# Attention slots: other places for splits, fillers and copies; last norm: gain and 1/rms in one operation

## The chip, the cores and the metric

The kernel runs on one core of one Trainium2 chip. The metric is the device time in microseconds (us), as the median of several runs. TensorE (PE) multiplies matrices into banks of PSUM. VectorE (DVE) and ScalarE (ACT) do the work by element, GpSimd (POOL) the reduction over partitions and some transfers, and SyncE (SP) starts most transfers. Each engine works through its own queue in order, and an instruction that waits holds up those behind it.

## The reference

A decoder trunk of two layers on 1024 tokens of width 1024, in f32. Layer 0 mixes by a short gated convolution, layer 1 by dilated attention with 16 heads of 64 and three branches. Each is followed by a SwiGLU, and a last RMSNorm ends it.

```python
def rms_norm(x, g):
    xf = x.astype(jnp.float32)
    y = xf * lax.rsqrt(jnp.mean(xf * xf, axis=-1, keepdims=True) + EPS)
    return (y * g.astype(jnp.float32)).astype(x.dtype)
...
    for i in range(DEPTH):
        h = rms_norm(x, mix_norm[i])
        j = i // N_MIXERS
        if i % N_MIXERS == 0:
            x = x + short_conv_mixer(h, conv_w_in[j], conv_kernel[j], conv_w_out[j])
        else:
            x = x + dilated_attention_mixer(h, attn_w_qkv[j], attn_w_out[j], rel_bias)
        h = rms_norm(x, ffn_norm[i])
        x = x + swiglu(h, ffn_w_gate[i], ffn_w_up[i], ffn_w_down[i])
    return rms_norm(x, final_norm)
```

In the attention, each branch (windows 128, 512 and 2048 at strides 1, 4 and 16) has scores q k / 8 plus a bias by distance, a softmax, and values. The branches are joined with weights by their sums of exponentials, which is the same as one softmax over the keys of all three.

## The kernel before, in words

Every f32 factor is split into two parts, hi and lo, and a product is three matmuls: hi hi, hi lo, lo hi (L372 to L374 in `product`). `split` makes the parts: ACT copies hi (L144), DVE subtracts for lo (L145).

The attention is a loop over 17 slots, n = 0 to 16. Slot n issues the scores of head n, the softmax of head n, the values of head n - 1, and 15 steps of a list of fillers, other matmuls that keep PE supplied. What is issued first stands first in each engine's queue: the order of the calls is the order of the work.

- `scores`: PE multiplies into seven banks (L1573, L1574). DVE adds the bias and writes the scores to four tiles, `lf`, `lh`, `ld` and `lp` (L1584, L1593, L1610, L1615), takes maxima into `m` (L1598 to L1624), and POOL reduces them over the partitions to `mb` (L1627).
- `softmax` has five steps, for lf, lh, ld and lp twice: DVE subtracts the maximum (L1635), ACT takes the exponential (L1636).
- `values` multiplies the exponentials by the values into two banks (L1646). The rows of one half hold the sums of exponentials: ACT takes their logarithm into `z` (L1669), and copies the rows of the other half into `o` (L1670).
- `finish` (for a pair of heads, two slots later) takes exp(-z) (L1677). `attended` multiplies o by it (L1710) and stores the page.
- The fillers stand in `FILL`: ("v", g) is a group of value tiles (L1516 to L1518, ACT copies with L1521), ("qk", g) is a pair of heads' projections. A result of a projection is emitted in four parts: DVE scales it into `kq` (L1139 or L1141), ACT copies `kq_hi` (L1144), DVE subtracts `kq_lo` (L1147). Behind the list stands the output product of the attended pages 0 to 3 (L372 to L374), which DVE adds to x (L491).
- In slot 12 (LAG - 1) these attended pages, loaded back as `oin`, are split by the generator `halves`, which the slot steps as `hook`.

PSUM has eight banks that are given out in turn, so the product that takes a bank waits until DVE or ACT has read what was put into it eight turns earlier.

The last norm runs in the kernel's last stage, on pieces of 512, 256 and 256 columns. `each` squares a tile on ACT and multiplies it by its gain on ACT (L1935). DVE adds the squares (L1940). When the sum of a piece is known, `scaled` multiplies each of the eight tiles by 1/rms on DVE (L1944) and stores it. For the last piece PE sums the squares (L1958), and spreads 1/rms over the partitions by a product with a diagonal (L1965, L1973): the last eight products read it from PSUM.

Of the kernel before, what the change touches and what calls it, by code (L numbers as in the profile page):

```python
# [12 lines left out]
AF = mybir.ActivationFunctionType  # L13
ALU = mybir.AluOpType
# [6 lines left out]
H = 16  # L21
KT = D // 128
FT = DF // 128
HALF = 512
# [22 lines left out]
SOFT = 4  # L47
# [1 line left out]
AO_WIDE = 5  # L49
AO = 4  # L50
LAG = 13
FILL = (("v", 0), ("v", 1), ("v", 2), ("qk", 6), ("qk", 7), ("v", 3))
DEEP_ORDER = (1, 2, 5, 6, 7, 3, 4)


# [39 lines left out]
def view(t, off, dims):  # L95
    return bass.AP(tensor=t.tensor, offset=t.offset + off, ap=[t.ap[0]] + [list(d) for d in dims])
# [3 lines left out]
def trunk(ctx: ExitStack, tc: tile.TileContext, x, gains_in, cwi, ck, cwo, wqkv, wo, relb,  # L100
          wg, wu, wd, oneh, ident, out):
    nc = tc.nc
# [6 lines left out]
    def page(name, dt=F32):  # L109
        return pages.tile([128, 1024], dt, name=name, tag="page", bufs=PAGES)  # L110
# [6 lines left out]
    def bank():  # L117
        return psum.tile([128, 512], F32, name="bank", tag="bank")

    def half(h):  # L120
        return slice(h * HALF, (h + 1) * HALF)
# [225 lines left out]
    add_units(QK, QK_PAIRS, lambda u, n: wqkv[(KT, 0)[n] + u])  # L347
    for kind, g in FILL:
        if kind == "v":
# [27 lines left out]
    def run(*gens):  # L377
        for _ in zip(*gens):
            pass
        for g in gens:  # L380
            for _ in g:
                pass
# [12 lines left out]
    X = [None] * KT  # L395
# [1068 lines left out]
    def load_bias(h):  # L1464
        t = scope["pool"].tile([128, L1 + L2], F32, name="bias", tag="bias", bufs=2)
        base = tables.offset + h * G3
        nc.sync.dma_start(t[:, 0:L1], bass.AP(tensor=tables.tensor, offset=base, ap=[[1, 8], [A1, 16], [1, L1]]))
        nc.sync.dma_start(t[:, L1:L1 + L2], bass.AP(tensor=tables.tensor, offset=base + G0,
                                                    ap=[[1, 32], [A2, 4], [1, L2]]))
        return t  # L1470
# [5 lines left out]
    def blk(j):  # L1476
        return (j // 4) * HALF + (j % 4) * 8

    def attention(norm, qk):
# [150 lines left out]
        def softmax(st):  # L1630
            lf, lh, ld, lp, mb = (st[n] for n in ("lf", "lh", "ld", "lp", "mb"))
            for dst, m in ((lf, mb), (lh, mb[:, HALF:]), (ld, mb),
                           (view(lp, 8, [[32, 16], [1, 24]]), view(mb, 8, [[32, 16], [1, 24]])),
                           (lp[:, HALF:], mb[:, HALF:])):
                nc.vector.tensor_tensor(out=dst, in0=dst, in1=m, op=ALU.subtract)  # L1635
                nc.scalar.activation(dst, dst, AF.Exp)  # L1636
                yield

        def values(p, a, st):
            lf, lh, ld, lp = (st[n] for n in ("lf", "lh", "ld", "lp"))  # L1640
            acc = [bank(), bank()]
            kd = [[128, 4], [1, 32]]
            b1 = [[32, 16], [1, 8]]

            def mm(ih, off, dims, u, rhs, first=False, last=False):
                nc.tensor.matmul(view(acc[ih], off, dims), vx[:, u, 64 * a:64 * a + 128], rhs,  # L1646
                                 start=first, stop=last)

            for ih in range(2):
                for r4 in range(4):  # L1650
                    mm(ih, r4 * 32, kd, 8 + r4, view(lf, ih * HALF + r4 * 32, kd), first=r4 == 0)
                    if r4 % 2:
                        yield
            for r4 in range(4):
                mm(1, r4 * 32, kd, 12 + r4, view(lh, r4 * 32, kd))
                if r4 % 2:
                    yield
            for j in range(8):
                off = (j % 4) * 8
                mm(j // 4, off, b1, j, view(ld, blk(j), b1), last=False)  # L1660
                if j:
                    mm(j // 4, off, b1, j - 1, view(lp, blk(j), b1), last=j % 4 == 3)
                yield
            o, z = st["o"], st["z"]
            n0 = slice(64 * a, 64 * a + 64)
            z0 = slice(64 - 64 * a, 128 - 64 * a)
            for ih in range(2):
                s = slice(ih * HALF, (ih + 1) * HALF)
                nc.scalar.activation(z[n0, s], acc[ih][z0], AF.Ln)  # L1669
                nc.scalar.activation(o[n0, s], acc[ih][n0], AF.Copy)  # L1670
            yield

        def finish(p):
# [42 lines left out]
        def slot(n, dense, ndense, late=0, hook=iter(())):  # L1716

            def other(k):
                for _ in range(k):
                    next(dense, None)  # L1720

            p, a = divmod(n, 2)
            if n < H:
                new = dict(bias=bias.pop(n))
                sc = scores(p, a, new)
            else:
                sc = iter(())
            if n + 1 < H:
                load_kq(n + 1)
                bias[n + 1] = load_bias(n + 1)  # L1730
            if n:
                q, b = divmod(n - 1, 2)
                if b == 0:
                    OZ[q] = page("o"), page("z")
                old = live.pop(n - 1)
                old.update(o=OZ[q][0], z=OZ[q][1])
                pv = values(q, b, old)
            else:
                pv = iter(())
            extra = later = iter(())  # L1740
            lagged = n <= LAG
            if n + 1 < H:
                later = classes(n + 1)
            if lagged and a and p:
                ending.append(finish(p - 1))
            used = 0
            if lagged:
                for i in range(8):
                    next(sc, None)
                    if n or i % 2:  # L1750
                        other(1)
                        used += 1
                    if a and ending and i == 0:
                        run(ending.pop())
                run(sc)
            else:
                if a == 0 and not late:
                    other(1)
                    used += 1
                for i in range(8):  # L1760
                    next(sc, None)
                    next(pv, None)
                    next(pv, None)
                    if i >= late and i % 2 == 0:
                        other(1)
                        used += 1
                run(sc)
                run(pv)
                if a == 0:
                    extra = finish(p - 1)  # L1770
                if a == 0 and n < H:
                    load_values(p)
            left = max(ndense - used, 0)
            for i in range(8):
                next(pv, None)
                next(pv, None)
                if i == (2 if n > LAG + 1 else 5):
                    attended()
                if not lagged and (i < FIN0 or i > SOFT):
                    next(extra, None)  # L1780
                if i in (1, 2):
                    next(later, None)
                if i == (3 if lagged else SOFT):
                    if n < H:
                        live[n] = new
                        run(softmax(new))
                if i >= SOFT:
                    next(hook, None)
                other(left * (i + 1) // 8 - left * i // 8)
            run(pv)  # L1790
            run(extra)

        def load_attended(ps):
# [29 lines left out]
        live = {}  # L1823
# [3 lines left out]
        def fill():  # L1827
            for kind, g in FILL[1:]:
                if kind == "qk":
# [65 lines left out]
    with tc.tile_pool(name="first", bufs=1) as scope["pool"]:  # L1895
# [4 lines left out]
        norm = Norm(1)  # L1900
        qk = QueryKey(norm)
# [12 lines left out]
    with tc.tile_pool(name="third", bufs=1) as scope["pool"]:  # L1914
# [3 lines left out]
        norm = Norm(4)  # L1918

        def final(key, ks, hid):  # L1920
            pieces = ((0, HALF), (HALF, 768), (768, S))
            sums, scale = [], []

            def each(n, c):

                s = slice(*c)
                if norm.acc is None:
                    norm.acc, norm.rstd = page("acc"), page("rstd")
                if n == 0:
                    nc.scalar.activation(norm.acc[:, s], X[n][:, s], AF.Square)  # L1930
                else:
                    sq = page("sq")
                    nc.scalar.activation(sq[:, s], X[n][:, s], AF.Square)
                    sums.append((sq, s))
                nc.scalar.activation(X[n][:, s], X[n][:, s], AF.Identity, scale=norm.gain(n))  # L1935

            def add_squares(keep=0):
                while len(sums) > keep:
# [2 lines left out]

            def scaled(i, n, rstd):
                s = slice(*pieces[i])
                nc.vector.tensor_tensor(out=X[n][:, s], in0=X[n][:, s], in1=rstd, op=ALU.mult)  # L1944
                (nc.sync, nc.scalar)[n % 2].dma_start(out[n][:, s], X[n][:, s])

            def some(k):
# [54 lines left out]
            rstd = spread(diag)  # L2002
            for n in range(KT):
                scaled(last, n, rstd)
# [52 lines left out]
```

## Time and profile before

| | before |
|---|---|
| median of 3 runs | 2121.59 us (2120.86 to 2122.68) |
| profiled execution | 2121.1 us |
| its span, first to last instruction | 2119.3 us |
| mean granted clock of PE | 0.997 |
| DVE, ACT and POOL busy | 82%, 48%, 11% of the span |

A row of the timeline has the start and the length in us, the engine, the line, the operation, what it writes <- what it reads, and the number of equal instructions joined in it; in brackets stands the idle time of the engine ahead of it, with what ended that. A row of a group has the total busy time in us behind the bar, and then the mean in ns. L12 is line 12 of the kernel before.

### The profile page before, as it was taken

The numbers are of one execution on the slowest core, as the hardware profiler recorded it, in microseconds if no ns is written. First come the engines' busy times: TensorE is split into PE (matmuls) and PEld (weight loads), VectorE is DVE, ScalarE is ACT, GpSimd is POOL, SyncE is SP. The second block draws the span as 40 slices with busy tenths as digits, with TensorE's granted clock in tenths as the row PEclk, the third lists the DMA queues.
The fourth block names the chain that finished last, engine by engine and source line by source line (L and its number), as shares of the span: only waits on it lengthen the run. The fifth ranks groups of instructions, "written<-read, shape, count | busy, mean of one in ns | idle before, by whom it ended". The sixth has DMA issues, their size and how long they took to land.

```text
span 2119.3 us, 30767 instructions
## 1 busy us (share of the span) xinstructions
PE 2088.8 (99%) x11006; PEld 1795.5 (85%) x11006; DVE 1737.2 (82%) x3255; ACT 1023.0 (48%) x1868; POOL 236.5 (11%) x337
## 2 busy tenths in 40 slices
PE   9999999999999999999999999899999999999998
PEld 7788888888888888887799999888788888888887
DVE  8898769988888888878967777786998888888876
ACT  7433427443444554446545555554544434456435
POOL 1000000110101000010322222111011001001000
PEclk9999999999999999999999999999999999999999
DMA  7322642333332576350867778855223323358432
GB/s 220 95 95 70 229 139 70 109 110 103 107 110 102 170 216 201 107 174 33 274 202 178 185 178 212 211 172 149 70 82 108 108 100 111 115 187 244 157 95 80
DMA packets 141527, 300.77 MB, mean 142 GB/s; under 512 B 48252, under 2 KB 54478, under 8 KB 141376
## 3 DMA queue, kind: packets, MB, share of 16 engines
q1 hardware_dynamic: 107488, 201.94, 32.3%
q0 software_dynamic: 26256, 82.18, 12.3%
q10 hardware_dynamic: 7632, 14.70, 1.8%
q8 instruction: 87, 1.43, 0.3%
q14 instruction: 64, 0.52, 0.1%
HBM read 208.49 MB, written 82.93 MB: 138 GB/s over the span
## 4 chain that ended last, share of the span: by engine, by line
PE 45%; DVE 5%; ACT 2%; issue 1%; POOL 1%; DMA 0%; SPq 0%; DVEq 0%; ACTq 0%; POOLq 0%
PE bank L572 8%; PE bank L570 8%; PE bank L571 8%; PE bank L1646 4%; PE bank L373 2%; PE bank L374 2%; PE bank L372 2%; PE bank L662 1%; PE bank L665 1%; PE bank L664 1%; PE bank L1516 1%; PE bank L1517 1%; PE bank L1518 1%; PE bank L1574 1%; PE bank L1573 1%
## 5 line engine op out<-in xcount | busy, mean ns | idle before, releaser
L572 PE MATMUL bank<-b,w 128*128 128x512 f32 x1952 | 760.9, 390 | 5.3 <-DVE w L145 5.0
L570 PE MATMUL bank<-b,w 128*128 128x512 f32 x1952 | 760.8, 390 | 3.5 <-ACT w L144 2.2
L571 PE MATMUL bank<-b,w 128*128 128x512 f32 x1952 | 760.4, 390 | 0.3 <-DVE b L881 0.3
L572 PEld LDWEIGHTS bank<-b,w 128*128 128x128 f32 x1952 | 366.4, 188 | 86.5 <-DVE w L145 10.4
L570 PEld LDWEIGHTS bank<-b,w 128*128 128x128 f32 x1952 | 366.6, 188 | 79.5 <-ACT w L144 3.1
L571 PEld LDWEIGHTS bank<-b,w 128*128 128x128 f32 x1952 | 366.6, 188 | 75.2 <-DVE b L881 1.4
L144 ACT ACTIVATE w<-combo 128x512 fp32r<-128x512 f32 (+2 forms) x488 | 249.7, 542 | 237.1 <-DVE combo L192 220.5
L145 DVE TENSOR_TENSOR w<-combo,w 128x512 fp32r<-128x512 f32 (+2 forms) x488 | 278.3, 584 | 37.8 <-ACT w L144 37.0
L576 ACT ACTIVATE part<-bank 128x512 f32<-128x512 f32 x186 | 110.9, 596 | 375.6 <-PE bank L572 375.2
L145 DVE TENSOR_TENSOR w<-raw,w 128x512 fp32r<-128x512 f32 (+2 forms) x342 | 189.9, 577 | 37.0 <-ACT w L144 37.0
L580 DVE TENSOR_TENSOR part<-part,bank 128x256 f32<-128x256 f32 (+1 forms) x366 | 171.9, 502 | 29.3 <-PE bank L572 16.6
L144 ACT ACTIVATE w<-raw 128x512 fp32r<-128x512 f32 (+2 forms) x342 | 167.3, 531 | 45.9 <-PE bank L572 12.2
L372 PE MATMUL bank<-w_hi,w 128*128 128x512 f32 (+1 forms) x400 | 151.1, 378 | 4.1 <-ACT w_hi L144 4.1
L373 PE MATMUL bank<-w_lo,w 128*128 128x512 f32 (+1 forms) x400 | 149.5, 374 | 1.5 <-DVE w_lo L145 1.5
L374 PE MATMUL bank<-w_hi,w 128*128 128x512 f32 (+1 forms) x400 | 149.5, 374 | 0.7 <-DVE w L145 0.7
L491 DVE TENSOR_TENSOR x<-x,bank 128x512 f32<-128x512 f32 (+1 forms) x104 | 66.5, 645 | 61.7 <-PE bank L374 60.8
L800 DVE TENSOR_TENSOR x<-x,bank 128x512 f32<-128x512 f32 x136 | 93.4, 687 | 28.2 <-PE bank L572 28.0
L192 DVE TENSOR_TENSOR combo<-raw 128x512 f32<-128x512 f32 (+1 forms) x172 | 111.8, 651 | 0.0
L372 PEld LDWEIGHTS bank<-w_hi,w 128*128 128x128 f32 x400 | 75.6, 189 | 17.0 <-ACT w_hi L144 4.5
L374 PEld LDWEIGHTS bank<-w_hi,w 128*128 128x128 f32 x400 | 75.5, 189 | 14.7 <-DVE w L145 1.6
L373 PEld LDWEIGHTS bank<-w_lo,w 128*128 128x128 f32 x400 | 75.7, 189 | 14.3 <-DVE w_lo L145 2.1
L563 DVE TENSOR_TENSOR b<-hin,b 128x512 fp32r<-128x512 f32 x126 | 79.7, 690 | 9.3 <-ACT b L562 9.2
(241 smaller groups left out, 3454.4 us busy)
## 6 DMA issues: line engine op xcount, KB each, us to landing
hin<-part SPq DMA_DIRECT2D x126, 256.0 KB
raw<-in_ffn_w_gate SPq DMA_DIRECT2D x44, 512.0 KB
raw<-in_ffn_w_up SPq DMA_DIRECT2D x44, 512.0 KB
part<-sum POOLq DMA_DIRECT2D x72, 256.0 KB, 2.3
raw<-in_ffn_w_down SPq DMA_DIRECT2D x48, 384.0 KB
raw<-in_attn_w_qkv SPq DMA_DIRECT2D x27, 512.0 KB
raw<-in_conv_w_in SPq DMA_DIRECT2D x24, 512.0 KB
part<-part POOLq DMA_DIRECT2D x36, 256.0 KB, 2.6
```

Source lines behind the costliest of these rows:

```text
L144: nc.scalar.activation(hi, src, AF.Copy)
L145: eng.tensor_tensor(out=lo, in0=src, in1=hi, op=ALU.subtract)
L192: eng.tensor_tensor(out=c, in0=a, in1=b, op=op)
L372: nc.tensor.matmul(b, whi[:, a], ahi[:, s], start=first, stop=False)
L373: nc.tensor.matmul(b, whi[:, a], alo[:, s], start=False, stop=False)
L374: nc.tensor.matmul(b, wlo[:, a], ahi[:, s], start=False, stop=last)
L570: nc.tensor.matmul(b, hi[:, a], bhi, start=start and k == 0, stop=False, skip_group_check=True)
L571: nc.tensor.matmul(b, hi[:, a], blo, start=False, stop=False, skip_group_check=True)
L572: nc.tensor.matmul(b, lo[:, a], bhi, start=False, stop=k == n - 1, skip_group_check=True)
L576: nc.scalar.activation(t, b, AF.Copy)
L580: nc.vector.tensor_tensor(out=t, in0=t, in1=b, op=ALU.add)
L800: nc.vector.tensor_tensor(out=X[n][:, half(h)], in0=X[n][:, half(h)], in1=b, op=ALU.add)
```

## The change

Four things are issued in another order, and one operation is joined:

- In FILL, ("v", 3) comes before ("qk", 7).
- `values` issues z and o of the first bank when that bank is complete (j = 3), and those of the second at j = 7, rather than all four after the loop.
- `slot` no longer runs the five steps of `softmax` at once, but one in each pass of its loop, between the steps of the values and the fillers.
- The hook is stepped in the first four passes, and so before the softmax and not after it.
- `each` has no product by the gain any more. `scaled` makes one scalar_tensor_tensor: 1/rms times gain times x.

```diff
-FILL = (("v", 0), ("v", 1), ("v", 2), ("qk", 6), ("qk", 7), ("v", 3))
+FILL = (("v", 0), ("v", 1), ("v", 2), ("qk", 6), ("v", 3), ("qk", 7))
...
+            o, z = st["o"], st["z"]
+            n0 = slice(64 * a, 64 * a + 64)
+            z0 = slice(64 - 64 * a, 128 - 64 * a)
             for j in range(8):
                 off = (j % 4) * 8
                 mm(j // 4, off, b1, j, view(ld, blk(j), b1), last=False)
                 if j:
                     mm(j // 4, off, b1, j - 1, view(lp, blk(j), b1), last=j % 4 == 3)
+                if j % 4 == 3:
+                    s = half(j // 4)
+                    nc.scalar.activation(z[n0, s], acc[j // 4][z0], AF.Ln)
+                    nc.scalar.activation(o[n0, s], acc[j // 4][n0], AF.Copy)
                 yield
-            o, z = st["o"], st["z"]
-            n0 = slice(64 * a, 64 * a + 64)
-            z0 = slice(64 - 64 * a, 128 - 64 * a)
-            for ih in range(2):
-                s = slice(ih * HALF, (ih + 1) * HALF)
-                nc.scalar.activation(z[n0, s], acc[ih][z0], AF.Ln)
-                nc.scalar.activation(o[n0, s], acc[ih][n0], AF.Copy)
             yield
...
-            extra = later = iter(())
+            extra = later = soft = iter(())
...
-                if i == (3 if lagged else SOFT):
-                    if n < H:
-                        live[n] = new
-                        run(softmax(new))
-                if i >= SOFT:
+                if i < 4:
                     next(hook, None)
+                if i == (3 if lagged else SOFT) and n < H:
+                    live[n] = new
+                    soft = softmax(new)
+                next(soft, None)
                 other(left * (i + 1) // 8 - left * i // 8)
             run(pv)
+            run(soft)
             run(extra)
...
-                nc.scalar.activation(X[n][:, s], X[n][:, s], AF.Identity, scale=norm.gain(n))
...
-                nc.vector.tensor_tensor(out=X[n][:, s], in0=X[n][:, s], in1=rstd, op=ALU.mult)
+                nc.vector.scalar_tensor_tensor(X[n][:, s], rstd, norm.gain(n), X[n][:, s], op0=ALU.mult, op1=ALU.mult)
```

The order of the instructions shows what this makes of each queue. First ACT in slot 12, before: the exponentials of head 12 (L1636), and behind them the splits of the attended pages, w_hi<-oin.

```order
860 L1557 ACTIVATE kca<-ka 128x512 x2
861 L1636 ACTIVATE lf<-lf 128x1024
862 L1636 ACTIVATE lh<-lh 128x512
863 L1636 ACTIVATE ld<-ld 128x1024
864 L1636 ACTIVATE lp<-lp 128x16x24
865 L1636 ACTIVATE lp<-lp 128x512
866 L144 ACTIVATE w_hi<-oin 128x1024
867 L1521 ACTIVATE v<-bank,scales 128x256
868 L144 ACTIVATE w_hi<-oin 128x1024 x2
```

The same place on ACT in the changed kernel (whose lines L1668 and L1669 are z and o):

```order
859 L144 ACTIVATE w_hi<-oin 128x1024
860 L1557 ACTIVATE kca<-ka 128x512
861 L144 ACTIVATE w_hi<-oin 128x1024
862 L1557 ACTIVATE kca<-ka 128x512
863 L144 ACTIVATE w_hi<-oin 128x1024 x2
864 L1636 ACTIVATE lf<-lf 128x1024
865 L1668 ACTIVATE z<-bank 64x512
866 L1669 ACTIVATE o<-bank 64x512
867 L1636 ACTIVATE lh<-lh 128x512
868 L1636 ACTIVATE ld<-ld 128x1024
869 L1144 ACTIVATE kq_hi<-kq 128x512
```

All four splits now stand ahead of the first exponential, and z, o and a kq_hi stand between the exponentials.

DVE in slot 12 of the changed kernel, from the last maxima of head 12 to the first bias of head 13 (L1584):

```order
1634 L1624 TENSOR_TENSOR m<-m,lp 128x512
1635 L145 TENSOR_TENSOR w_lo<-oin,w_hi 128x1024 x4
1636 L1635 TENSOR_TENSOR lf<-lf,mb 128x1024
1637 L1635 TENSOR_TENSOR lh<-lh,mb 128x512
1638 L1141 SCALAR_TENSOR_TENSOR kq<-bank,rstd 128x512
1639 L1635 TENSOR_TENSOR ld<-ld,mb 128x1024
1640 L1147 TENSOR_TENSOR kq_lo<-kq,kq_hi 128x512
1641 L1635 TENSOR_TENSOR lp<-lp,mb 128x16x24
1642 L1635 TENSOR_TENSOR lp<-lp,mb 128x512
1643 L1584 TENSOR_TENSOR lf<-bank,bias 128x4x64 x4
1644 L491 TENSOR_TENSOR x<-x,bank 128x512
```

Before, the four w_lo stood behind the five subtractions, and there was no kq in this slot.

ACT in slot 1, as a difference: the splits of raw value weights (w_hi<-raw), and the exponentials, z and o of heads 1 and 0 around them.

```order
 L1636 ACTIVATE lf<-lf 128x1024
-L1636 ACTIVATE lh<-lh 128x512
-L1636 ACTIVATE ld<-ld 128x1024
-L1636 ACTIVATE lp<-lp 128x16x24
-L1636 ACTIVATE lp<-lp 128x512
 L144 ACTIVATE w_hi<-raw 128x1024
-L1669 ACTIVATE z<-bank 64x512
-L1670 ACTIVATE o<-bank 64x512
-L1669 ACTIVATE z<-bank 64x512
-L1670 ACTIVATE o<-bank 64x512
+L1668 ACTIVATE z<-bank 64x512
+L1669 ACTIVATE o<-bank 64x512
```

Four exponentials that were ahead of the split now stand behind it, and behind the first z and o.

## The prediction

> **What bounds the kernel now.** The page of the profile comes first: its span, and each engine's busy time.
>
> ```profile
> span 2119.3 us, 30767 instructions
> PE 2088.8 (99%) x11006; PEld 1795.5 (85%) x11006; DVE 1737.2 (82%) x3255; ACT 1023.0 (48%) x1868; POOL 236.5 (11%) x337
> ```
>
> TensorE (PE) is busy for all but 30.5 us of the span, and the change leaves its matmuls alone. So a gain can only come from idle PE time and from time at a lower clock. The second view lists what PE waited for: the line waited for, then us in total, times, and the longest.
>
> ```profile
> PE bank L372 <- ACT w_hi L144: 4.1, 2, 3.7
> PE bank L1573 <- ACT o L1670: 2.7, 3, 1.1
> PE bank L1958 <- DVE acc L1940: 2.1, 1, 2.1
> PE bank L373 <- DVE w_lo L145: 1.5, 2, 0.8
> PE bank L1973 <- DVE diag L1965: 1.0, 1, 1.0
> ```
>
> These five rows are 11.4 us, and all end in work that the change touches: the splits of attended pages (L144 and L145), the copies of o (L1670) and the last norm. The third view shows stretches of time: length, then busy us of PE, PEld, DVE, ACT and POOL, then the granted clock.
>
> ```profile
> 1140.00:1160.00 20.00, 18.43 (x157) 18.02 (x155) 15.65 (x31) 9.65 (x15) 5.26 (x5) 1.00 0.62 149
> 1340.00:1360.00 20.00, 14.42 (x79) 12.14 (x77) 13.88 (x23) 13.72 (x18) 2.17 (x4) 0.91 0.63 141
> 1346.00:1349.40 3.40, 3.13 (x11) 2.87 (x12) 2.58 (x3) 2.57 (x5) 1.79 (x4) 0.51 0.61 151
> ```
>
> The worst place of the attention is slot 12: PE is busy for 14.42 of 20 us, and for 3.4 us the clock stands at 0.51. The fourth view, the timeline, tells why.
>
> ```profile
> 1339.02 1.23 DVE L1635 TENSOR_TENSOR lf<-lf,mb 128x1024 f32<-128x1024 f32 x1 [3.44 <-POOL mb L1627]
> 1340.28 1.06 ACT L1636 ACTIVATE lf<-lf 128x1024 f32<-128x1024 f32 x1 [4.86 <-DVE lf L1635]
> 1342.99 1.03 ACT L1636 ACTIVATE lp<-lp 128x384 f32<-128x384 f32 x2
> 1343.92 1.04 ACT L144 ACTIVATE w_hi<-oin 128x1024 fp32r<-128x1024 f32 x1
> 1345.01 0.51 PE L372 MATMUL bank<-w_hi,w 128*128 128x512 f32 x1 [3.73 <-ACT w_hi L144]
> 1346.27 0.79 PE L373 MATMUL bank<-w_lo,w 128*128 128x512 f32 x1 [0.75 <-DVE w_lo L145]
> 1351.58 0.50 PE L372 MATMUL bank<-w_hi,w 128*128 128x512 f32 x1 [0.33 <-ACT w_hi L144]
> 1352.84 0.50 PE L373 MATMUL bank<-w_lo,w 128*128 128x512 f32 x1 [0.77 <-DVE w_lo L145]
> ```
>
> The first w_hi<-oin stands behind all five exponentials on ACT, which itself had sat idle for 4.86 us before them. The slow clock begins 1.0 us behind the 3.73 us gap.
>
> **Slot 12.** The hook now runs before the softmax, so on ACT the four w_hi come ahead of the exponential of lf. They take 4 x 1.04 = 4.2 us and fit into the idle 4.86 us, or nearly so: one of the two kca copies now stands among them. PE wants the first at 1345.01 - 3.73 = 1341.28, and it will be there. The four waits are 3.73 + 0.75 + 0.33 + 0.77 = 5.58 us. The slow stretch costs (1 - 0.51) x 3.40 = 1.7 us more, and should go with the gap. **Term: -7.3**; if the two waits for w_lo stay, it is -5.8.
>
> The row shows the clock falling once, behind the longest gap of the attention. [...]
>
> **Slot 13, a wait that is added.** DVE now makes the four w_lo ahead of the softmax's subtractions, and two emissions of the moved projections ("qk", 7) fall into slot 12: one among the maxima, one between lh and ld.
>
> ```profile
> 1344.99 3.67 DVE L145 TENSOR_TENSOR w_lo<-oin,w_hi 128x1024 fp32r<-128x1024 f32 x3 [1.94 <-ACT w_hi L144]
> 1341.90 1.16 DVE L1635 TENSOR_TENSOR lp<-lp,mb 128x384 f32<-128x384 f32 x2
> L1141 DVE SCALAR_TENSOR_TENSOR kq<-bank,rstd 128x512 f32<-128x512 f32 x4 | 2.7, 684 | 0.0
> L1147 DVE TENSOR_TENSOR kq_lo<-kq,kq_hi 128x512 fp32r<-128x512 f32 x8 | 6.2, 769 | 3.6 <-ACT kq_hi L1144 3.6
> 1360.54 0.68 DVE L491 TENSOR_TENSOR x<-x,bank 128x512 f32<-128x512 f32 x1
> 1361.53 1.72 PE L1646 MATMUL bank<-lf,vx 128*128 128x128 f32 x14
> ```
>
> A split costs 3.67 / 3 = 1.22, four 4.9; an emission 0.68 + 0.77 = 1.45. Before, DVE was free at 1339.02 - 3.44 = 1335.58 and waited for POOL. Now it has the first emission and then the splits: 1335.58 + 1.45 + 4.9 = 1341.9 for the subtraction of lf, 2.9 later than before. (The wait for POOL is filled by the splits.) The subtractions ended at 1343.06 (1341.90 + 1.16); now that becomes 1343.06 + 2.9 + 1.45 = 1347.4. From the last w_lo, for which PE waited until 1352.84, to the end of the second L491 (1361.22), DVE took 8.4 us, of which I take 1.1 as small waits on PE that go. So L491 now ends between 1347.4 + 7.3 = 1354.7 and 1355.8, and I take 1355.9, since kq_lo also has to wait for kq_hi on ACT. That L491 releases the bank that the values (L1646) take next; before, it was done 0.31 us ahead of them. PE, 7.3 us earlier, arrives at 1361.53 - 7.3 = 1354.2. It waits 1355.9 - 1354.2 = **+1.7** (0.5 to 2.3, by the two ends with half a microsecond for the waits).
>
> **Slots 9 and 10.** The order of fillers takes the four emissions of ("qk", 7), eight operations on DVE, away from here, and o is copied sooner.
>
> ```profile
> 1288.53 1.06 ACT L1636 ACTIVATE lf<-lf 128x1024 f32<-128x1024 f32 x1 [2.42 <-DVE lf L1635]
> 1292.77 0.59 ACT L1670 ACTIVATE o<-bank 64x512 f32<-64x512 f32 x1
> 1293.41 0.38 PE L1573 MATMUL bank<-qa,ka 128*128 128x256 f32 x1 [1.14 <-ACT o L1670]
> ```
>
> The first z and o follow the exponential of lf directly: done by about 1289.5 + 2 x 0.6 = 1290.7 rather than 1293.36. The gap of 1.14 goes. The second bank is copied between the exponentials of ld and lp, where up to 0.3 may be left. **Term: -0.8** (-1.14 to 0).
>
> **Slots 1 to 3.** Here the split softmax has a price. In slot 1 a split of the value weights stands between two exponentials and two subtractions, on both engines, and z and o push the exponentials back.
>
> ```profile
> 1140.71 1.23 DVE L145 TENSOR_TENSOR w_lo<-raw,w_hi 128x1024 fp32r<-128x1024 f32 x1 [1.87 <-ACT w_hi L144]
> 1158.78 0.39 PE L1573 MATMUL bank<-qa,ka 128*128 128x256 f32 x1 [1.10 <-ACT o L1670]
> 1160.02 0.38 PE L1573 MATMUL bank<-qa,ka 128*128 128x256 f32 x1 [0.49 <-ACT o L1670]
> 1161.83 0.38 PE L1573 MATMUL bank<-qa,ka 128*128 128x256 f32 x1 [0.33 <-ACT v L1521]
> ```
>
> DVE already waited 1.87 for the second w_hi, which on ACT comes behind the same exponentials, z, o and v as before, but these now start behind a DVE that has done a w_lo between lf and lh. A w_lo takes 1.2 on DVE, so w_hi and all of slot 2 are up to 1.2 later; I take 1.1. In slot 3 the early copies free their banks in time, but the last gap is ended by v, on an ACT that has as much ahead of it as before. So PE's waits don't go: 1.10 + 0.49 + 0.33 = 1.92 becomes about 3.0. **Term: +1.1**, from -1.9 (they all go) to +2.4 (two such delays). I add **+0.3** for slots 4 to 8 and 11, where the same pattern meets a DVE with 3.4 us idle per slot (0 to +1.1).
>
> **The last norm.** ACT loses the 24 operations of L1935, and DVE's 24 products become three-operand ones.
>
> ```profile
> L1935 ACT ACTIVATE x<-x,gains 128x256 f32<-128x256 f32 x16 | 8.2, 512 | 0.5
> L1252 DVE SCALAR_TENSOR_TENSOR hcol<-x,gains,rstd x16: 743/749/758, 317.0 to 1478.3; 128x512 f32<-128x512 f32 x16
> L1282 DVE TENSOR_TENSOR x<-x,rstd x16: 683/694/701, 341.8 to 1502.2; 128x512 f32<-128x512 f32 x16
> 2105.48 0.42 DVE L1944 TENSOR_TENSOR x<-x,rstd 128x256 f32<-128x256 f32 x1 [1.56 <-ACT rstd L487]
> 2109.22 0.42 DVE L1940 TENSOR_TENSOR acc<-acc,sq 128x256 f32<-128x256 f32 x1
> 2113.02 2.74 DVE L1944 TENSOR_TENSOR x<-x,bank 128x256 f32<-128x256 f32 x8
> ```
>
> L1252 has exactly the new form (tile, gain per partition, tile): 749 against 694 ns, +0.055 each. At 2105.48 DVE had waited 1.56 for 1/rms, and on ACT three or four of the 0.51 us operations stood ahead of it: it comes about 1.5 earlier. From there DVE runs back to back to 2109.64, so PE's wait of 2.12 (L1958) shrinks by 1.5 less 4 x 0.055, about 1.3. The end has 12 more products, four from SBUF and eight from PSUM: 12 x 0.055 = +0.66. **Term: -0.7**, from -1.3 to +0.6 (nothing gained, only the operations' cost).
>
> [...]
>
> **Sum.** -7.3 + 1.7 - 0.8 + 1.1 + 0.3 - 0.7 = -5.7 us, on the profiled execution's 2121.1 us: 2115.4. That execution lies 0.5 below the median of 2121.59, so the forecast is **2115.9**. From the median, the best ends give -7.3 + 0.5 - 1.14 - 1.9 + 0 - 1.3 = -11.1, 2110.5; the worst -5.8 + 2.3 + 0 + 2.4 + 1.1 + 0.6 = +0.6, 2122.2.
>
> **The rivals.**
>
> *DVE takes the gain back in slot 13 (22%).* If kq_lo in slot 12 waits for a kq_hi behind z, o and exponentials, DVE is 2 us later than reckoned, and PE waits 3.7 at L1646, as long as the old gap, with its 1.7 of slow clock: 2115.9 + 2.0 + 1.7 = 2119.6. For it: DVE and ACT are both busy 13.9 and 13.7 of 20 us there already. Against: ACT has 4.86 us of room ahead of the exponentials, and the splits fill it.
>
> *The attention's loop gets longer (14%), the slower side.* The chain that ended last runs through DVE, POOL and ACT from slot 3 to slot 9, and in it kq_hi stands behind an exponential.
>
> ```profile
> 1241.38 3.23 POOL mb L1627
> 1247.63 1.06 ACT ld L1636
> 1249.53 0.62 ACT kq_hi L1144
> ```
>
> Now z and o, 2 x 0.6 us, stand between the exponentials and ahead of many a kq_hi. If each of the eight emissions (the 8 of L1147) holds DVE up by 1.2 us, that is 9.6, and if one of PE's waits grows to the 3.7 us of slot 12 with it, 1.7 of slow clock. It reaches PE only where DVE has no reserve left. The forecast already holds 0.3 of it: 2115.9 + 9.6 + 1.7 - 0.3 = 2126.9. It decides from 5.7 + 4.2 = 9.9 us on that reach PE. Against it: DVE waits for POOL by 3.44 us in a slot, which takes up such delays, and of the three waits of L1573 for o none lies between 1160.02 and 1293.41.
>
> *All the stalls go (11%).* If slot 1's delay is absorbed by the same waits for POOL, slot 3 has no gap either, and DVE is early in slot 13: the best ends, 2110.5. For it: 3.44 is more than 1.2. Against: DVE waited 1.87 for just that w_hi.
>
> *The attended pages come too late (4%), so that the hook does not do what it is for.* The loads of oin wait for pages that the moved projections now hold for longer. If they land later than the exponential of lf once began, w_hi stops ACT as long as before: the term of -7.3 is lost, 2123.2. Against: the first w_hi followed the last exponential at once, so its page had been there before 1343.92; how long before, no row here shows.
>
> [...]
>
> **How the numbers follow.** The forecast has 46%, and the rivals 22, 14, 11, 4 and 3. About 0.2% (4.2 us) is what a measurement of this kernel can tell from no change: faster means below 2117.4, slower above 2125.8. Of the forecast's own range, 2110.5 to 2122.2, more than four fifths by weight lie below 2117.4, since only the slots 1 to 3 term is wide: 38 of its 46 points are faster. With the 11 of the third rival and 4 of the first, that is 0.53. Same: 8 + 18 + 3 + 3 = 0.32. Slower: the 14 of the loop and 1 of the late pages, 0.15. The range goes from 2110.5 (all the stalls) to 2124.5, past the first and the fourth rival; it leaves out the loop and a little below.
>
> **What would show it.** Slot 12: no wait of L372 for w_hi, ACT's first w_hi<-oin ahead of the exponential of lf, and no stretch below full clock before the end. Slot 13: a wait of L1646 for DVE's L491 of 0.5 to 2.3 us. Around the former 1293: no wait of L1573 for o. Slot 3: a wait of L1573 for v, about 3 us in all. Last norm: L1944 at about 0.47 us for 256 columns and 0.75 for 512, and a wait at L1958 below 1 us. The forecast is wrong if PE's waits in slots 12 and 13 together exceed 4 us, if new waits of L1573 or L1646 appear in slots 4 to 11, or if the clock falls somewhere else in the attention.

## The result and the profile after

| | before | changed |
|---|---|---|
| median of 12 runs each | 2121.92 us (2120.80 to 2123.68) | 2115.60 us (2113.87 to 2117.24) |
| profiled execution, its span | 2121.1, 2119.3 us | 2115.11, 2113.3 us |

The ratio is 0.9971 (95% interval 0.9964 to 0.9979): faster by 6.3 us, where 5.7 was forecast. The sum came out; several of its terms didn't, and one reason for the gain was missing from it.

The waits of PE in the attention and the last norm of the changed kernel, as line waited for, us in total, times and longest (L1668 and L1669 are now z and o; rows of the other stages are left out):

```profile
PE bank L1573 <- ACT o L1669: 1.5, 1, 1.5
PE bank L1958 <- DVE acc L1940: 1.3, 1, 1.3
PE bank L1973 <- DVE diag L1965: 1.0, 1, 1.0
PE bank L1573 <- DVE lf L1584: 0.9, 1, 0.9
PE bank L1516 <- ACT v L1521: 0.8, 1, 0.8
PE bank L1573 <- ACT v L1521: 0.7, 2, 0.3
PE bank L372 <- ACT v L1521: 0.5, 1, 0.5
PE bank L1646 <- ACT lf L1636: 0.3, 1, 0.3
```

The waits for w_hi and w_lo are gone. Those in slot 3 are not: the timeline of PE has three, 1.53 + 0.83 + 0.33 = 2.69 us where there were 1.92.

```profile
1159.60 0.38 PE L1573 MATMUL bank<-qa,ka 128*128 128x256 f32 x1 [1.53 <-ACT o L1669]
1161.17 0.39 PE L1516 MATMUL bank<-w_hi,b 128*128 128x256 f32 x1 [0.83 <-ACT v L1521]
1162.48 0.45 PE L1573 MATMUL bank<-qa,ka 128*128 128x256 f32 x1 [0.33 <-ACT v L1521]
```

In stretches of time (length, busy us of PE, PEld, DVE, ACT and POOL, granted clock), PE is now busy through slot 12 at full clock; the slow stretch of the attention stands behind slot 3:

```profile
1159.25:1162.66 3.41, 1.90 (x11) 1.49 (x12) 3.38 (x9) 3.36 (x7) 0.00 (x0) 1.00 0.51 138
1162.66:1166.08 3.42, 3.42 (x17) 3.42 (x18) 2.30 (x6) 1.86 (x2) 0.45 (x1) 0.50 0.43 109
1334.00:1354.00 20.00, 19.97 (x132) 17.92 (x131) 17.75 (x27) 13.27 (x18) 6.22 (x5) 1.00 1.05 266
```

The span is 6.0 us shorter. By the gaps on PE that is: slot 12 -5.58 of waits and -1.7 of slow clock; slot 14 +0.31; slot 10 -0.22 (0.92 for 1.14); slot 3 +0.77 of waits and +1.7 of slow clock; slot 5 +0.79 (two waits for v); behind the attention -1.4; the start of the kernel, which the change leaves alone, -0.35. These make -5.7; the rest lies in gaps under 0.25 us.

### The profile page after: what moved, and what is told of

Read it like the earlier page. It is cut to its first block, busy times and chain, and to the rows that moved or that the text cites. A ratio compares the mean times of both kernels' runs of the same rounds, so it can differ in the third digit from the quotient of the medians.

```text
span 2113.3 us, 30743 instructions
## 1 busy us (share of the span) xinstructions
PE 2088.5 (99%) x11006; PEld 1795.8 (85%) x11006; DVE 1739.6 (82%) x3255; ACT 1008.0 (48%) x1844; POOL 236.8 (11%) x337
## 5 line engine op out<-in xcount | busy, mean ns | idle before, releaser
L491 DVE TENSOR_TENSOR x<-x,bank 128x512 f32<-128x512 f32 (+1 forms) x104 | 66.3, 643 | 59.9 <-PE bank L374 59.1
```

## The experiments

The first theory: the hook carries the gain, the split softmax costs some of it in slots 1 to 3, and the last norm adds about 1 us. The rivals: the split softmax with the early copies of z and o carries it, or the order of the fillers does. All kernels were timed in five rounds beside the kernel before; ratios are to that, with 95% intervals.

**The hook alone, on the kernel before.**

```diff
+                if i < 4:
+                    next(hook, None)
                 if i == (3 if lagged else SOFT):
...
-                if i >= SOFT:
-                    next(hook, None)
```

> The kernel before with one edit alone: the hook is stepped in the first four passes of the slot, ahead of the softmax. Theory (the hook carries the gain): the four waits of slot 12, 5.58 us, and the slow stretch behind them, 1.7 us, go; slot 13 may get up to 1.7 us of a new wait. 2121.9 - 7.3 + 0.3 to 1.7 = 2114.9 to 2116.3, as fast as the whole change without the last norm's 1.4. Rival (the split softmax with the early copies is needed for it, since the splits of the pages only push the exponentials of slot 12 back): the wait moves to the values of slot 13 and the time stays at 2120 to 2122.

Measured: 2117.91 us, ratio 0.9979 (0.9971 to 0.9988). The hook alone is faster, but by less than the theory gave. The timeline shows why: the waits of slot 12 are gone, and in slot 13 the values wait.

```profile
1357.73 2.52 PE L1646 MATMUL bank<-lf,vx 128*128 128x128 f32 x16 [2.51 <-DMA vx<-vdram]
```

Not DVE is late there, as the prediction had it, but the values of the last heads, which come back from DRAM. The profile has slow stretches of 3.4 us behind this wait and behind slot 3.

**The hook and the fillers' order, on the kernel before.** The hook's edit is the one above; with it goes this line:

```diff
-FILL = (("v", 0), ("v", 1), ("v", 2), ("qk", 6), ("qk", 7), ("v", 3))
+FILL = (("v", 0), ("v", 1), ("v", 2), ("qk", 6), ("v", 3), ("qk", 7))
```

> The kernel before with two edits, the hook ahead of the softmax and the change's order of the fillers. The hook alone left a wait of 2.51 us in slot 13 for the load of the last group's values, vx<-vdram, and a slow stretch behind it. Theory (the order of the fillers is what takes this wait away, since the last value tiles are stored two slots sooner): it goes with its slow stretch, 2117.9 - 2.5 - 1.7 = 2113.7, and the waits of slot 3 stay. Rival (the load is late for another reason, because the queues of DMA are full there): the wait stays, 2117 to 2118.

Measured: 2112.82 us, ratio 0.9960 (0.9947 to 0.9972). The wait for vx is gone, and in the attention only the waits of slot 3 are left, 1.91 us. The wait of 1.14 in slot 10 went as well. By the medians, two edits of five bring more than the whole change (0.9971); the intervals overlap.

**The changed kernel with the fillers as before** (the same lines, the other way round).

> The changed kernel with the fillers in the order of before. Theory (the order is what has the last group's values back in time for slot 13): L1646 waits in slot 13 for vx<-vdram by 2 to 2.5 us, now and then with a slow stretch, and slot 10 has its wait for o again: 2115.6 + 2 to 4 = 2117.6 to 2119.6. Rival (the split softmax makes PE late enough in slot 13 for the load): 2115 to 2116.

Measured: 2120.28 us, ratio 0.9994 (0.9986 to 1.0003), 0.7 above the expected range. Here the chain can be read, in the timelines of ACT, POOL, SP and PE:

```profile
1349.50 0.47 ACT L1521 ACTIVATE v<-bank,scales 128x256 f32<-128x256 f32 x1
1350.27 2.17 POOL L1525 DMA_DIRECT2D vdram<-v  x4 [6.90 <-ACT v L1521]
1354.87 0.38 SPq L1533 DMA_DIRECT2D vx<-vdram  x1
1359.01 3.37 PE L1646 MATMUL bank<-lf,vx 128*128 128x128 f32 x15 [2.57 <-DMA vx<-vdram]
```

The last v tile is copied at 1349.50, stored, loaded back, and PE waits 2.57 us for it, with a slow stretch behind. The old order of fillers puts the last tile into slot 12. In the kernel before, the same copy was at 1344.87 and PE came to these values only at 1361.53, so the load was in time. Without the fillers' order next to nothing of the whole change's gain is left; the hook alone, above, gains 4.5 us, with the same kind of wait.

**The fillers' order alone, on the kernel before** (the one line of FILL).

> The kernel before with the fillers' order of the change alone. Theory (the order is worth much only with the hook, since before the values were back in time anyway, behind the stall of slot 12): the wait of 1.14 us in slot 10 goes, the waits of slot 12 stay at 5 us or more with their slow stretch: 2121.6 - 1.1 = 2120.5, within 1 us. Rival (the order is worth its 4 us by itself, because it relieves DVE in slots 8 to 10): 2117 to 2118.

Measured: 2120.96 us, ratio 0.9993 (0.9984 to 1.0002), no change that can be told. The list of waits has 1.1 us less for o, as expected, and more for w_hi:

```profile
PE bank L372 <- ACT w_hi L144: 5.1, 2, 4.6
PE bank L1573 <- ACT o L1670: 1.6, 2, 1.1
```

What slot 10 gains is lost in slot 12, where one wait is now 4.60 us. By the medians, the order alone brings about 1 us (which its interval can't tell from none) and the hook alone 4.5; together they bring 8.5.

**The changed kernel with the hook back behind the softmax's start.**

```diff
-                if i < 4:
-                    next(hook, None)
...
+                if i >= SOFT:
+                    next(hook, None)
                 next(soft, None)
```

> The changed kernel with the hook back in the passes from SOFT on. Theory (the hook carries the gain): the waits of L372 and L373 in slot 12 come back with 5 us or more, since z, o and the exponentials now stand between the splits too, and there are two slow stretches, in slot 3 and in slot 12: 2115.6 + 5 to 9 = 2120.6 to 2124.6. Rival (the gain comes from the split softmax and the early copies): at most 1 us more, 2115.6 to 2116.6.

Measured: 2131.68 us, ratio 1.0046 (1.0033 to 1.0058): the theory's side, and 7 us beyond its range. PE waits in the timeline, and the clock in the stretches:

```profile
1349.42 0.79 PE L372 MATMUL bank<-w_hi,w 128*128 128x512 f32 x1 [3.44 <-ACT w_hi L144]
1359.20 0.80 PE L372 MATMUL bank<-w_hi,w 128*128 128x512 f32 x1 [3.83 <-ACT w_hi L144]
```

```profile
1349.15:1366.21 17.06, 11.45 (x30) 7.84 (x31) 10.07 (x14) 9.02 (x13) 1.10 (x2) 0.50 0.61 146
```

The split softmax and the split pages now take turns on ACT and DVE, each waiting for the other. The waits add up to 3.44 + 0.47 + 3.83 + 0.46 + 0.47 = 8.7 us, and the clock stays at half speed for 17.06 us, where I had allowed one stretch of 3.4 in this slot.

**The changed kernel with the softmax at once again.**

```diff
-                    soft = softmax(new)
-                next(soft, None)
+                    run(softmax(new))
```

> The changed kernel with the five steps of the softmax run at once again. Theory (the split softmax costs in slot 1 and slot 3): the second w_hi of slot 1 is 1.1 us earlier, the waits in slot 3 fall from 2.69 to 1.9 us or less, and the slow stretch behind them goes, as it was absent in the kernel before with 1.92 us of waits: 2115.6 - 0.8 - 1.7 = 2113.1. The wait of 0.8 us in slot 5 may go too, 2112.3. Rival (the split softmax is needed to free the banks early): waits of L1573 for o come back, 1 to 3 us more, 2116.6 to 2118.6.

Measured: 2113.15 us, ratio 0.9960 (0.9947 to 0.9972), as the theory had it. Waits of slot 3: 1.88 us, no slow stretch behind them; slots 5 and 10: none. New are 0.45 in slot 13 and 0.92 in slot 14. By the medians, then, undoing the split of the softmax makes the changed kernel about 2.5 us faster; the intervals, 0.9947 to 0.9972 and 0.9964 to 0.9979, overlap a little.

**The changed kernel with z and o copied after the loop.**

```diff
-                if j % 4 == 3:
-                    s = half(j // 4)
-                    nc.scalar.activation(z[n0, s], acc[j // 4][z0], AF.Ln)
-                    nc.scalar.activation(o[n0, s], acc[j // 4][n0], AF.Copy)
                 yield
+            for ih in range(2):
+                s = half(ih)
+                nc.scalar.activation(z[n0, s], acc[ih][z0], AF.Ln)
+                nc.scalar.activation(o[n0, s], acc[ih][n0], AF.Copy)
             yield
```

> The changed kernel with z and o of both banks copied after the loop again, behind the exponentials. Theory (the early copies bring nothing on their own, since in slot 3 the wait only moves from o to v, and the banks of the other slots are free in time): the waits of slot 3 stay between 1.9 and 2.7 us, the wait of slot 10 is for o again, 2115.6 with at most 1 either way. Rival (the early copies are what lets the split softmax pass): the waits for o grow by 1.2 us in each of slots 3, 5 and 10, 2118 to 2120.

Measured: 2120.13 us, ratio 0.9993 (0.9984 to 1.0002). The theory fails here and the rival holds in the time, though not in slot 3, where no wait for o over 0.25 us is left. The list of waits:

```profile
PE bank L1573 <- ACT o L1670: 5.2, 6, 1.8
PE bank L1573 <- ACT v L1521: 0.8, 3, 0.3
```

With the steps of the softmax spread over the slot, copies that stand behind the loop stand behind all of it, and o is late in slots 2, 5, 10 and 13. The early copies pay for what the split softmax would cost; without the split (the hook and the fillers' order, above) they aren't needed.

**The last norm as before, in the changed kernel.** L1935 (Identity by the gain) is put back, and L1944 is a tensor_tensor again.

> The changed kernel with the last norm as before: the product by the gain on ACT, a two-operand product on DVE. Theory (the joined operation takes ACT's work out of the way of 1/rms and of the sums' split, and costs 0.06 on DVE): L485 and L1958 wait longer again by 0.6 and 0.85, less 0.2 for the cheaper products at the end, 2115.6 + 1.3 = 2116.9. Rival (the end is set by the last products and the stores, so that the longer products cancel the gain): 2115.2 to 2115.9.

Measured: 2117.96 us, ratio 0.9983 (0.9974 to 0.9992), against 0.9971 for the whole change: +2.4 us, where 1.3 was expected, and with intervals that overlap. Not all of it need be the norm's: in the profiled execution the slow stretch behind slot 3 lasts 6.8 us, for 3.4 in the changed kernel's.

**The last norm alone, on the kernel before.** The product by the gain is gone from `each`, and `scaled` has the joined operation.

> The kernel before with the last norm's edit alone. Theory (ACT's product by the gain stood ahead of the splits of the sums and of 1/rms): the waits of L485, 0.6 us, and 0.85 of the wait of L1958 go, the twelve longer products at the end give back up to 0.2 to 0.7: 2121.6 - 0.8 to 1.3 = 2120.3 to 2120.8. Rival (the longer products and the stores cancel it): 2121.6 and no change of the span behind 2090.

Measured: 2119.78 us, ratio 0.9992 (0.9983 to 1.0001), 1.8 us less, where the interval only just reaches no change. The wait behind it is the clearer evidence: L1957 here is L1958 of before.

```profile
PE bank L1957 <- DVE acc L1939: 1.3, 1, 1.3
```

Every kernel with the joined operation has 1.3 there, every other 2.1.

**Slot 3 cleared, in the changed kernel:** the softmax is whole in slot 1, and in slot 2 starts in the last pass.

```diff
-                if i == (3 if lagged else SOFT) and n < H:
+                if i == (7 if n == 2 else 3 if lagged else SOFT) and n < H:
                     live[n] = new
                     soft = softmax(new)
+                if n == 1:
+                    run(soft)
                 next(soft, None)
```

> The changed kernel with the softmax whole in slot 1 alone, and started in the last pass in slot 2, so that z, o and v of slot 2 stand ahead of its exponentials on ACT, which sat idle for 8.6 us there. Theory: slot 3 loses its three waits, 2.69 us, and the slow stretch behind them, 1.7 us: 2115.6 - 4.4 = 2111.2. Rival (the waits of slot 3 come from a DVE and POOL that are late as a whole, so that only the name of the wait changes): a wait of 1.5 to 2.7 us for DVE or for an exponential takes their place, 2113.5 to 2115.6.

Measured: 2110.66 us, ratio 0.9947 (0.9933 to 0.9961). No wait is left in slot 3. The timeline of ACT shows z and o in what was idle time ahead of the exponentials:

```profile
1149.05 0.59 ACT L1668 ACTIVATE z<-bank 64x512 f32<-64x512 f32 x1 [2.70 <-PE bank L1646]
1152.87 0.59 ACT L1669 ACTIVATE o<-bank 64x512 f32<-64x512 f32 x1
1154.29 1.06 ACT L1636 ACTIVATE lf<-lf 128x1024 f32<-128x1024 f32 x1 [0.82 <-DVE lf L1635]
```

In the changed kernel the second bank's o was done at 1159.55 in this slot, here at 1153.46.

**The softmax split from slot 12 on only**, with slot 2 as above (`if n < LAG - 1: run(soft)` in place of `n == 1`).

> The changed kernel with the softmax whole in slots 0 to 11, started in the last pass in slot 2, and split from slot 12 on. Theory: the waits of slots 3, 5 and 10 are gone with the split softmax there (2.69, 0.80 and 0.92 us), those of slots 13 and 14, which the kernel with the softmax whole throughout had (0.45 and 0.91 us), do not come, so only 0.3 us of waits are left in the attention: 2110.7 - 1.6 = 2109.1. Rival (the waits of slots 5 and 10 come from the early copies and the order of the fillers and not from the split): the same as with slots 1 and 2 alone, 2110.7.

Measured: 2109.58 us, ratio 0.9947 (0.9934 to 0.9959). The waits of slots 5 and 10 are gone with the split, as the theory had it; waits of 0.60 and 0.34 us are left behind slot 12.

**The hook, the fillers' order and the last norm alone, with slot 2's softmax last.** Of the edits only the new one, for slot 2, is shown:

```diff
-                    if n < H:
+                    if n < H and n != 2:
...
             run(pv)
+            if n == 2:
+                live[n] = new
+                run(softmax(new))
             run(extra)
```

> The kernel before with the hook, the fillers' order and the last norm of the change, without the split softmax and without the early copies, and with the softmax of slot 2 behind z, o and v. Theory (two of the change's five edits and the norm carry all of the gain, the rest costs): the waits of slot 3, 1.91 us, go, and those of L485 and L1958 shrink by 1.4: 2112.8 - 1.9 - 1.2 = 2109.7, no wait over 0.3 us in the attention, as fast as the version with the softmax whole up to slot 11 or up to 1 us faster. Rival (the waits of slot 3 move into slot 4 or 5 when the exponentials of slot 2 are late): 2111 to 2113.

Measured: 2107.92 us, ratio 0.9934 (0.9920 to 0.9948), 13.7 us faster than before, 1.8 below the 2109.7 expected, and the lowest median of all; its interval overlaps those of the two kernels above. PE has no gap over 0.25 us in the attention any more. Its longest waits are outside:

```profile
PE bank L572 <- DVE w L145: 5.6, 6, 2.3
PE bank L1960 <- DVE acc L1942: 1.3, 1, 1.3
PE bank L570 <- ACT w L144: 1.2, 2, 0.6
```

## Why the prediction was right, point by point

**Slot 12 (-7.3): right in mechanism and size.** The gaps and their slow stretch went, 5.58 + 1.7 us. The hook alone shows that it is the hook.

**Slot 13 (+1.7): wrong; measured nothing there, and 0.31 in slot 14 for an exponential.** The step that failed is the bank: the second L491 does not release what the values take next. It ran when the values had been going for 2.9 us without a wait:

```profile
1356.31 1.95 PE L1646 MATMUL bank<-lf,vx 128*128 128x128 f32 x16
1359.22 0.68 DVE L491 TENSOR_TENSOR x<-x,bank 128x512 f32<-128x512 f32 x1
```

That it had been done 0.31 us ahead of the values before was a coincidence. DVE was also later than reckoned, without harm: the subtraction of lf came at 1345.38, not 1341.9, since DVE came free 2.1 us later and the splits took 1.4 longer. What the first rival supposed came about, a DVE that waits 2.19 us in slot 12 for a kq_hi behind z, o and exponentials; but since that L491 holds no bank for the values, it cost PE nothing. The wait that the earlier PE really meets in slot 13 is the one for vx, and the prediction doesn't name it; the fillers' order, which takes it away, was counted at -0.8 for slot 10 alone. Within the changed kernel it is worth 4.7 us by the medians (2120.28 against 2115.60).

**Slots 9 and 10 (-0.8): measured -0.22.** The wait for o went, but one of 0.92 us for a bias addition of DVE (L1584) took its place. With the softmax at once it is gone, so the split makes DVE late there: in both kernels a split of value weights has DVE wait for its w_hi (3.59 us here, 3.53 with the softmax at once), but only here do the subtractions of ld and lp stand behind it.

**Slots 1 to 3 (+1.1): right in the delay, wrong in the wait, short by the clock.** The second w_hi of slot 1 came 1.1 us later, relative to a start that was 0.35 us earlier, and the three waits grew to 2.69, by 0.77. Before, and changed:

```profile
1139.63 1.05 ACT L144 ACTIVATE w_hi<-raw 128x1024 fp32r<-128x1024 f32 x1
1140.35 1.05 ACT L144 ACTIVATE w_hi<-raw 128x1024 fp32r<-128x1024 f32 x1
```

But the early copies did not free their banks in time, as the prediction had it: the longest of the three waits, 1.53 us, is still for o, since the exponentials of lh and ld stand ahead of the second bank's copy. Nor was it foreseen that a slow stretch of 3.4 us follows these waits in the profiled execution, 1.7 us more. How much of that the median holds isn't known: with the fillers as before, the same three waits (1.53, 0.83 and 0.32 us) were followed by full clock.

**The other slots (+0.3): measured +0.79**, both waits in slot 5 for v.

**The last norm (-0.7): the term was mis-sized.** PE's shift against before grew from -4.65 us ahead of the norm to -6.0 at the end, -1.35. The wait of L1958 shrank by 0.84, not 1.3. Two things were not in the sum. The product before, L485, had waited 0.6 us for the split of the sums on ACT, behind an operation of L1935, and that wait went too. And the last twelve products cost DVE +0.72, as reckoned with +0.66 (3.22 for 2.74 and 1.66 for 1.42 us), but little of it is in the span: L1973 starts 6.19 us earlier than before, and the span ends 6.03 earlier. From the end of the last product to the end of the span, where the last stores run, it took 3.1 us, for 3.6 before. The product's price held also from PSUM. The last of the five chances, 3%, stood for a far dearer product, and no run shows one: it took 746 ns for 512 columns (690 before), 478 for 256 (420), 472 from PSUM (417).

```profile
2107.02 3.22 DVE L1944 SCALAR_TENSOR_TENSOR x<-bank,gains,x 128x256 f32<-128x256 f32 x8
L1944 DVE SCALAR_TENSOR_TENSOR x<-rstd,gains,x 128x512 f32<-128x512 f32 x8 | 6.0, 746 | 1.4 <-ACT rstd L487 1.4
L1944 DVE SCALAR_TENSOR_TENSOR x<-bank,gains,x 128x256 f32<-128x256 f32 x8 | 3.2, 472 | 0.0
```

So the total was met by luck, by terms that cancel: 1.4 too much cost in slots 13 and 14, 0.7 too little gain for the norm, 0.6 too good in slot 10, 1.4 too good in slots 1 to 3 and 0.5 in slot 5. Several of the prediction's own signs of being wrong appeared: the clock fell in slot 3, L1573 had new waits in slots 5 (0.34 us) and 10 (0.92), and L1958 still waited 1.28 us, not less than 1.

Of the rivals, the longer loop is in the kernel, with 0.79 us in slot 5 and 0.92 in slot 10, far below its price of 11.0. The late attended pages did not come about; the late values did, in the two kernels that have the hook and not the fillers' order.

## What to carry to other kernels

When a stall goes, follow every input of the work behind it, loads through DRAM included: what arrived during the stall was in time only because of it. Two edits can be worth more together than apart (here 8.5 us against 4.5 and 1), so an edit that looks like nothing in the profile before has to be priced at the place that the other edit creates. And interleaving two chains that pass between ACT and DVE made each wait for the other here; whole pieces of work in an engine's idle time did better.

## What the runs showed of the hardware

**The clock also fell where no wait was longer than 1.53 us.** In the changed kernel's profiled execution a stretch at half speed (granted clock 0.50) begins at 1162.663 and lasts 3.413 us. The longest wait of PE ahead of it, in slot 3, was 1.53 us, and PE had been busy for 1.90 of the last 3.41 us. In the kernel before, one of 3.413 us begins at 1346.047, behind the gap of 3.73 in slot 12. Slot 3 of that kernel, with three waits of 1.92 us in all, was followed by full clock. Two rows of the kernel before, over most of slot 3's waits and ahead of the slow stretch:

```profile
1158.31:1161.73 3.42, 2.23 (x14) 1.82 (x14) 3.35 (x9) 3.35 (x7) 0.00 (x0) 1.00 0.83 209
1342.63:1346.05 3.42, 0.51 (x1) 0.19 (x1) 1.49 (x2) 3.42 (x6) 0.43 (x1) 1.00 0.01 2
```

In each of the two executions a second slow stretch, which lasts to the end, begins in the last norm, at 2104.742 and at 2110.632. In both the granted clock is 0.50 from there on. The same part of the code with nearly the same waits shows both outcomes, first the hook alone and then the hook with the fillers' order:

```profile
1157.70:1161.10 3.40, 1.82 (x13) 1.42 (x13) 3.37 (x10) 3.30 (x7) 0.00 (x0) 1.00 1.01 289
1161.10:1164.50 3.40, 3.40 (x17) 3.40 (x18) 2.55 (x7) 3.40 (x5) 0.00 (x0) 0.50 0.32 76
```

```profile
1157.70:1161.10 3.40, 1.82 (x14) 1.41 (x12) 3.37 (x9) 3.30 (x7) 0.00 (x0) 1.00 1.01 258
1161.10:1164.50 3.40, 3.07 (x26) 2.87 (x25) 3.14 (x8) 3.25 (x4) 0.00 (x0) 1.00 0.36 75
```

PE is busy for 1.82 us of 3.40 in both, and only the first is followed by half speed. What decides between the two is not shown.

**Splits ran longer beside a reduction, and in slot 12 the reduction too.** In slot 12 of the changed kernel the four w_lo ran while POOL reduced over the partitions:

```profile
1339.13 6.32 DVE L145 TENSOR_TENSOR w_lo<-oin,w_hi 128x1024 fp32r<-128x1024 f32 x4
1339.39 4.05 POOL L1627 PARTITION_ALL_REDUCE mb<-m  x1 [1.86 <-DVE m L1624]
```

The reduction took 4.05 us, for 3.21 to 3.23 in the other fifteen slots of this execution, and the four splits 6.32 for the 4.9 reckoned from the row before. The kernel with the hook back has the two apart in the same slot, and there neither is longer:

```profile
1341.45 3.22 POOL L1627 PARTITION_ALL_REDUCE mb<-m  x1 [1.86 <-DVE m L1624]
1349.40 1.23 DVE L145 TENSOR_TENSOR w_lo<-oin,w_hi 128x1024 fp32r<-128x1024 f32 x1 [3.46 <-ACT w_hi L144]
```

In slot 6 of the changed kernel two splits of weights, of the same size, took 3.46 us beside a reduction, for 1.21 to 1.23 each in the slots ahead of it, and there the reduction stayed at 3.22. When the reduction itself gets longer is not shown.
